# GpSimd makes every other low part at the end of each layer of a two-layer encoder

## Chip, cores and metric

The kernel runs on one core of one Trainium2 chip. The metric is the device time of one execution in microseconds (us). Three runs of the kernel before gave 1799.69, 1801.23 and 1801.38 us: the median is 1801.23 us. The trace is of one further execution, which took 1798.99 us.

## What is computed

Two encoder layers act on x, 256 tokens of 1024 channels. In each, a token mixer (two attention branches, gates, an output projection) is added to x, and then a product-key expert layer (PEER) is added to x. The PEER layer is what matters here:

```
u = expert_down[eidx]; vv = expert_up[eidx]          # 128 experts of 16384 for each token
act = gelu(einsum('td,thkd->thk', xc, u))
out = einsum('thk,thkd->td', g * act, vv)             # g: softmax over the chosen scores
x = x + out
```

The second layer starts with `rms_norm(x, norm_mix[1])` and the projection `h @ w_in[1]`, so it needs x complete.

## The kernel before

**Units.** All weights go through one stream (class `Stream`, line 156) of 602 units of 128 x 1024 float32, 301 for each layer: 66 of projections, 128 of expert_down, and 107 blocks of expert_up. I number the blocks of a layer by k, from 0 to 106; block k is unit up0 + k. A block is 128 rows of expert_up, ordered by need, and `blocks_of` (line 332) lists which of the two halves of the tokens (chunks 0 and 1) use it: blocks 90 to 98 serve both, blocks 99 to 106 serve chunk 1 alone.

**Parts.** Every unit is split in two parts, because a float32 product is made of three products of reduced parts. `_prep` (line 191) is the life of a unit: wait for its data `raw`; ScalarE (ACT) copies it into the high part `wh` (line 199); then the low part `wl = raw - wh` is made (line 203), by VectorE (DVE), or by GpSimd (POOL) where the flag `gpsimd` is set, which it is during the top-k stage; then the load of a later unit is asked for. `wh` and `wl` have 4 buffers each, so the parts of block k + 4 wait until TensorE (PE) is done with block k.

```
        engine, req = ((self.nc.vector, ("v", 1.14)), (self.nc.gpsimd, ("g", 2.5)))[self.gpsimd]   # line 200
        t = yield req
        ...
        self.splits.append(engine.tensor_sub(lo, r, h.bitcast(F32)).ins.name)
        ...
        self.load(u + self.depth)
```

**Loads.** A block of expert_up is gathered by an indirect DMA that GpSimd issues (`rows`, line 1272). Four blocks of ten land in `raw` buffers, six in free stretches of the tile `act`. `depth` is 10 during the blocks and goes back to 4 (`AHEAD`) at k = 87 (line 1461), so from then on the gather of block k + 4 is the next thing in the program after the low part of block k.

**Blocks.** `block` (line 1389) does, for each chunk, six matmuls of 512 columns (line 1401): two of the activations' high part with `wh`, two of it with `wl`, two of the activations' low part with `wh`. The activations' parts come from `split_rows`: high by ScalarE (line 1288), low by VectorE (line 1290). In front of block 97 stands `make_up` (line 1411): a block under `tc.If` for the rare rows that were missed. Every engine reads a flag there (line 1416) and branches; the body isn't entered in these runs. After block 98 chunk 0 is complete, and `norm_lane` (line 379) adds it to x and normalizes it for the next layer (lines 387, 390, 393, 397, 400, 357 to 360, 406), with a transpose on TensorE (line 368) and two parts of the result (lines 372 and 374). The last three blocks, 104 to 106, run in half-blocks of three matmuls: first all three for columns 0 to 511, then all three for columns 512 to 1023. Then comes `first_half` (line 462) of the next layer, or, in the last layer, `store_lane` (line 409).

**Order.** Each engine executes its instructions in program order. The program order is set while the kernel is built: the class `Lanes` (line 71) keeps one clock for each engine and lets generators ("lanes") emit their next instruction when the clock of that engine is near enough to TensorE's; each `yield ("v", 1.14)` is a cost on an engine's clock. SyncE (SP) issues the plain loads.

Of the kernel before, what the change touches and what calls it, by code (L numbers as in the profile page):

```python
# [70 lines left out]
class Lanes:  # L71
# [8 lines left out]
    def __init__(self):  # L80
        self.clk = {"p": 0.0, "v": 0.0, "s": 0.0, "g": 0.0}
        self.lanes = []
        self.stuck = 0
        self.urgent = 0
# [71 lines left out]
class Stream:  # L156


    def __init__(self, nc, pool, srcs, lanes):
        self.nc, self.pool, self.srcs, self.lanes = nc, pool, srcs, lanes  # L160
        self.raw, self.parts, self.ready = {}, {}, {}
        self.nd = self.np = self.want = 0
        self.ahead = self.depth = AHEAD
        self.gpsimd = False
        self.busy, self.pooled, self.splits = set(), [], []
        self.rows = None

# [23 lines left out]
    def _prep(self, u):  # L191
        self.load(u)
        while u not in self.raw:
            yield None
            self.load(u)
        yield ("s", 0.97)
        r = self.raw.pop(u)
        h = self.pool.tile([128, UNIT], F32R, name="wh", bufs=AHEAD)
        self.nc.scalar.activation(h, r, AF.Copy)  # L199
        engine, req = ((self.nc.vector, ("v", 1.14)), (self.nc.gpsimd, ("g", 2.5)))[self.gpsimd]  # L200
        t = yield req
        lo = self.pool.tile([128, UNIT], F32R, name="wl", bufs=AHEAD)
        self.splits.append(engine.tensor_sub(lo, r, h.bitcast(F32)).ins.name)  # L203
        self.ready[u] = t - 0.05
        self.parts[u] = (h, lo)
        self.busy.discard(u)
        self.load(u + self.depth)
# [19 lines left out]
def encoder_kernel(ctx, tc, x_in, wts, downs, ups, gains, gate_bias, qk_norm, rpb, sink, skeys, consts, sums, out,  # L227
# [91 lines left out]
    def bcast_row(src, off, n):  # L319
        return bass.AP(tensor=src.tensor, offset=src.offset + off, ap=[[0, 128], [1, n]])  # L320
# [3 lines left out]
    def preload(func):  # L324
        nc.scalar.activation(tiny[:, 1:2], tiny[:, 0:1], func)  # L325
# [6 lines left out]
    def blocks_of(l):  # L332


        seq = []
        for r, (_, _, cap, ea, sb) in enumerate(LISTS):
            both = [(l, r, b, (0, 1)) for b in range(sb, ea)]
            one = [(l, r, b, (0,)) for b in range(sb)] + [(l, r, b, (1,)) for b in range(ea, cap)]
            if r:
                seq += [(l, None, i, (0, 1)) for i in range(WHOLE[0], sum(WHOLE))]  # L340
                one, end = one[:sb], one[sb:]
            while both or one:
                for x in (both, one):
                    if x:
                        seq.append(x.pop(0))
        return seq + end
# [6 lines left out]
    st = Stream(nc, wpool, srcs, lanes)  # L353
# [25 lines left out]
    def norm_lane(ch, adds, gain, xn, key, halves=(0, 1)):  # L379

        sc = nst[:, ch]
        for k in halves:
            c = slice(k * 512, (k + 1) * 512)
            xs = x[:, ch, c]
            if adds:
                yield ("v", vcost(512))
                nc.vector.tensor_add(xs, xs, adds[k])
                give(adds[k], "a")
            yield ("s", scost(512))
            nc.scalar.activation(xn[:, c], xs, AF.Square, accum_out=sc[:, k:k + 1])  # L390
            if k == 0:
                yield ("v", 0.1)
                nc.vector.tensor_scalar(sc[:, 2:3], sc[:, 0:1], 1.0 / D, EPS, op0=OP.mult, op1=OP.add)
        if halves[-1] == 0:
            return
        yield ("v", 0.15)
        nc.vector.scalar_tensor_tensor(sc[:, 3:4], sc[:, 1:2], 1.0 / D, sc[:, 2:3], op0=OP.mult, op1=OP.add)
        lanes.urgent += 2
        yield ("s", 0.2)
        nc.scalar.activation(sc[:, 4:5], sc[:, 3:4], AF.Sqrt)  # L400
        yield ("v", 0.8)
        newton(sc[:, 3:4], sc[:, 4:5], sc[:, 5:6], sc[:, 6:7])
        for k in range(2):
            c = slice(k * 512, (k + 1) * 512)
            t = yield ("v", 0.68)
            nc.vector.scalar_tensor_tensor(xn[:, c], x[:, ch, c], sc[:, 4:5], gain[:, c], op0=OP.mult, op1=OP.mult)
            lanes.add(transposed_parts(ch, k, xn[:, c], key, t), first=True)

    def store_lane(ch, k, acc):
        c = slice(k * 512, (k + 1) * 512)  # L410
        yield ("v", vcost(512))
        nc.vector.tensor_add(x[:, ch, c], x[:, ch, c], acc)  # L412
        give(acc, "a")
        nc.sync.dma_start(out[ch * 128:(ch + 1) * 128, c], x[:, ch, c])
# [57 lines left out]
    u = 0  # L472
    acc_first = None

    for l in range(depth):
# [858 lines left out]
        up0 = u + 12 + 128  # L1334
        seq = blocks_of(l)
# [53 lines left out]
        def block(n, ch, halves=(0, 1), last=False):  # L1389
            h, lo = st.get(n)  # L1390
            main_need(("ga", n))
            v = ring[n]
            w = slice(ch * 128, (ch + 1) * 128)
            lh, ll = v[:, 0, w], v[:, 1, w]
            first = [(ch, hf) not in begun for hf in range(2)]
            begun.update((ch, hf) for hf in halves)

            def emit():
                for a, r in ((lh, h), (lh, lo), (ll, h)):
                    for hf in halves:  # L1400
                        nc.tensor.matmul(oacc[ch][hf], a, r[:, hf * 512:(hf + 1) * 512],  # L1401
                                         start=first[hf] and a is lh and r is h, stop=last and a is ll)

            main(emit, 0.705 * len(halves), n)

        def next_split(n):

            if n < up0 + len(seq):
                lanes.add(split_rows(n, halves_of(TTf, 4 + n % 4)), prio=1)
# [32 lines left out]
        for k, (_, r, b, chs) in enumerate(seq[:-TAIL]):  # L1442
            if k == last[0] - 1:
                make_up()
            for ch in chs:
                block(u, ch, last=k == last[ch])
            if k == 60 and l + 1 < depth:
                nc.sync.dma_start(afl[:, 0:D], bcast_row(gains, 2 * (l + 1) * D, D))
            if k == last[0]:
                preload(AF.Sqrt)  # L1450
                for x_ in [x_ for x_ in done if x_[0] == "T1"]:
                    del done[x_]
                if l + 1 < depth:
                    lanes.add(norm_lane(0, oacc[0], afl[:, 0:D], afl[:, D:2 * D], "T1"), first=True)
                else:
                    for hf in range(2):
                        lanes.add(store_lane(0, hf, oacc[0][hf]), first=True)
            if k == 1:
                st.ahead = AHEAD
            if k == len(seq) - 20:  # L1460
                st.depth = AHEAD
            st.finish(u)
            u += 1
            next_split(u + 2)
# [109 lines left out]
```

## Time and profile before

| what | value |
|---|---|
| median of 3 runs | 1801.23 us |
| the profiled execution | 1798.99 us |
| its span, first to last instruction | 1797.2 us |
| TensorE busy | 1771.5 us (99% of the span) |
| VectorE busy | 1438.8 us (80%) |
| ScalarE busy | 1096.4 us (61%) |
| GpSimd busy | 577.5 us (32%) |
| low parts made by VectorE / by GpSimd | 570 / 32 |

All times of the trace are microseconds from the start of the span. A row of the timeline is one instruction, or several alike (x4) that follow each other: start, duration of all, engine, line of the kernel, operation, output and inputs. In square brackets stands the idle time of the engine in front of it and what ended that. Matmuls overlap, so the duration of a row can reach into the next one. Layer 0 ends near 904 us, layer 1 near 1793 us.

### The profile page before, as it was taken

The page shows a single profiled execution, that of the slowest core. Times are in us where ns is not written, and L with a number is a line of the kernel's source. Part 1 is how long each engine was busy: PE and PEld are TensorE (multiplying, and loading weights), DVE is VectorE, ACT ScalarE, POOL GpSimd, SP SyncE. Part 2 cuts the span into 40 slices and gives each one's busy share as a digit, 9 for nine tenths or more (in the row PEclk, how much of TensorE's full clock was granted, in tenths as well). Part 3 has the DMA queues.
Part 4 walks back from the last instruction along what each step waited for, and adds up shares of the span by engine and source line. Part 5 has one row for each costly group of instructions (what it writes and reads, how often), then busy time and mean ns, then how long its engine had stood idle before and what let it go on. Part 6 is the DMA issues. An engine that isn't in the chain of part 4 may idle for free. (4 is left out here: it accounts for less than half of the span.)

```text
span 1797.2 us, 38047 instructions
## 1 busy us (share of the span) xinstructions
PE 1771.5 (99%) x14646; PEld 1634.2 (91%) x14646; DVE 1438.8 (80%) x3278; ACT 1096.4 (61%) x1788; POOL 577.5 (32%) x480
## 2 busy tenths in 40 slices
PE   8999999999999999999999999999999999999998
PEld 7889899999999998888778998999999999988886
DVE  6986799988878967776689768999888788677665
ACT  5675545666667646665646755556666676466654
POOL 0000160000037867755200003500000577677551
PEclk9999999999999999999999999999999999999999
DMA  7535556544458879998664355565444677899983
GB/s 262 162 106 170 160 155 190 174 143 153 143 179 251 237 243 353 358 337 287 200 211 145 112 167 164 155 186 176 142 147 152 192 243 237 253 358 357 322 286 133
DMA packets 130519, 377.42 MB, mean 210 GB/s; under 512 B 17552, under 2 KB 43792, under 8 KB 130320
## 3 DMA queue, kind: packets, MB, share of 16 engines
q1 hardware_dynamic: 90288, 239.28, 43.6%
q0 software_dynamic: 40032, 135.54, 20.7%
q8 instruction: 119, 1.95, 0.5%
q14 instruction: 80, 0.66, 0.1%
HBM read 342.00 MB, written 32.75 MB: 209 GB/s over the span
## 5 line engine op out<-in xcount | busy, mean ns | idle before, releaser
L203 DVE TENSOR_TENSOR wl<-raw,wh 128x1024 fp32r<-128x1024 f32 x444 | 541.7, 1223 | 141.6 <-ACT wh L199 131.6
L199 ACT ACTIVATE wh<-raw 128x1024 fp32r<-128x1024 f32 x476 | 502.6, 1057 | 217.8 <-PE bank L1401 58.5
L1367 PE MATMUL bank<-TT,wh 128*128 128x256 f32 x2048 | 592.0, 289 | 0.0
L1368 PE MATMUL bank<-TT,wh 128*128 128x256 f32 x2048 | 578.9, 283 | 0.0
L1369 PE MATMUL bank<-TT,wl 128*128 128x256 f32 x2048 | 578.4, 282 | 0.0
L1368 PEld LDWEIGHTS bank<-TT,wh 128*128 128x128 f32 x2048 | 392.1, 191 | 0.0
L1369 PEld LDWEIGHTS bank<-TT,wl 128*128 128x128 f32 x2048 | 391.9, 191 | 0.0
L1367 PEld LDWEIGHTS bank<-TT,wh 128*128 128x128 f32 x2048 | 391.5, 191 | 0.3
L1401 PE MATMUL bank<-wh,TT 128*128 128x512 f32 x1296 | 349.2, 390 | 3.4 <-DVE TT L1290 2.2
L1212 POOL DMA_INDIRECT rows<-act,rank x240 | 278.1, 1159 | 114.7 <-issue 60.3
L1401 PEld LDWEIGHTS bank<-wh,TT 128*128 128x128 f32 x1296 | 242.6, 188 | 56.6 <-DVE TT L1290 4.7
L888 POOL IOTA act<- 128x128 uint32 (+2 forms) x6 | 2.0, 332 | 890.5 <-PE bank L368 408.7
L203 DVE TENSOR_TENSOR wl<-act,wh 128x1024 fp32r<-128x1024 f32 x126 | 154.3, 1225 | 77.7 <-ACT wh L199 77.5
L1401 PE MATMUL bank<-wl,TT 128*128 128x512 f32 x648 | 200.8, 389 | 1.0 <-issue 1.0
L199 ACT ACTIVATE wh<-act 128x1024 fp32r<-128x1024 f32 x126 | 133.6, 1061 | 96.8 <-PE bank L1401 87.9
L1272 POOL DMA_INDIRECT act<-in_ups_dram,act x118 | 130.8, 1108 | 89.4 <-DVE TT L1290 36.7
L1401 PEld LDWEIGHTS bank<-wl,TT 128*128 128x128 f32 x648 | 121.6, 188 | 26.7 <-issue 1.4
L448 PE MATMUL bank<-TT,wh 128*128 128x256 f32 x448 | 130.1, 290 | 1.5 <-ACT raw_ka L577 1.0
L450 PE MATMUL bank<-TT,wh 128*128 128x256 f32 x448 | 126.6, 283 | 0.0
L451 PE MATMUL bank<-TT,wl 128*128 128x256 f32 x448 | 126.6, 283 | 0.0
L1072 ACT ACTIVATE oh<-oh 128x1024 f16<-128x1024 f16 (+2 forms) x108 | 101.4, 955 | 11.5 <-DVE oh L1069 10.4
L1109 ACT ACTIVATE act<-bank 128x288 f32<-128x288 f32 (+31 forms) x152 | 52.2, 347 | 92.0 <-PE bank L1096 87.8
(268 smaller groups left out, 2936.6 us busy)
## 6 DMA issues: line engine op xcount, KB each, us to landing
raw<-in_downs_dram SPq DMA_DIRECT2D x256, 512.0 KB, 3.8
raw<-in_wts_dram SPq DMA_DIRECT2D x132, 512.0 KB, 4.1
act<-rows SPq DMA_DIRECT2D x100, 129.0 KB, 5.2
act<-rows SPq DMA_DIRECT2D x98, 64.5 KB, 5.2
act<-in_ups_dram SPq DMA_DIRECT2D x8, 512.0 KB, 7.5
raw<-in_ups_dram SPq DMA_DIRECT2D x8, 512.0 KB, 6.2
rows<-act,rank POOLq DMA_INDIRECT x240
act<-in_ups_dram,act POOLq DMA_INDIRECT x118
```

Source lines behind the costliest of these rows:

```text
L199: self.nc.scalar.activation(h, r, AF.Copy)
L203: self.splits.append(engine.tensor_sub(lo, r, h.bitcast(F32)).ins.name)
L448: nc.tensor.matmul(o, wh, rh, start=first and i == 0 and pc == 0, stop=False, skip_group_check=True)
L450: nc.tensor.matmul(o, wh, rl, start=False, stop=False, skip_group_check=True)
L451: nc.tensor.matmul(o, wl, rh, start=False, stop=last and i == len(kcs) - 1 and pc == 1, skip_group_check=True)
L1072: nc.scalar.activation(el, ej, AF.Copy, scale=LOW)
L1212: snd = nc.gpsimd.indirect_dma_start(byrank[r], bass.IndirectOffsetOnAxis(ap=rank[:, i:i + 1], axis=0), afl[:, i * ROW:(i + 1) * ROW], None)
L1272: nc.gpsimd.indirect_dma_start(w, None, ups_rows, bass.IndirectOffsetOnAxis(ap=num, axis=0), element_offset=l * 16384 * D)
L1367: nc.tensor.matmul(o, lh, TT[:, :, 0, kc, :], start=kc == 0, stop=False)
L1368: nc.tensor.matmul(o, lh, TT[:, :, 1, kc, :], start=False, stop=False)
L1369: nc.tensor.matmul(o, ll, TT[:, :, 0, kc, :], start=False, stop=kc == 7)
L1401: nc.tensor.matmul(oacc[ch][hf], a, r[:, hf * 512:(hf + 1) * 512], start=first[hf] and a is lh and r is h, stop=last and a is ll)
```

## The change

```diff
@@ class Stream: __init__
         self.gpsimd = False
+        self.also = set()
@@ class Stream: _prep
-        engine, req = ((self.nc.vector, ("v", 1.14)), (self.nc.gpsimd, ("g", 2.5)))[self.gpsimd]
+        engine, req = ((self.nc.vector, ("v", 1.14)), (self.nc.gpsimd, ("g", 2.5)))[self.gpsimd or u in self.also]
@@ the loop over the blocks of expert_up
             if k == len(seq) - 20:
                 st.depth = AHEAD
+
+                st.also |= set(range(up0 + len(seq) - 10, up0 + len(seq) + 3, 2))
             st.finish(u)
```

`len(seq)` is 107. In layer 0 the set holds the units of blocks 97, 99, 101, 103 and 105 and the first and third unit of layer 1, which continue the numbers as 107 and 109: seven low parts go from VectorE to GpSimd. In layer 1 it holds blocks 97, 99, 101, 103 and 105; units 107 and 109 don't exist there. Nothing else is edited.

## Rows read from the trace of the kernel before

**Rows 1.** Busy time by stretch: sum of PE, PEld, DVE, ACT, POOL.

```profile
890.00:910.00 20.00, 16.65 (x72) 12.14 (x71) 17.42 (x33) 12.95 (x27) 0.00 (x0) 1.00 0.41 131
1700.00:1760.00 60.00, 60.00 (x267) 49.69 (x266) 39.65 (x53) 35.70 (x54) 33.78 (x30) 1.00 0.87 289
1760.00:1797.20 37.20, 31.62 (x136) 24.90 (x134) 21.18 (x31) 17.41 (x27) 3.10 (x3) 0.97 0.28 99
```

**Rows 2.** Timeline of TensorE where layer 0 ends: its waits.

```profile
896.70 1.32 PE L368 MATMUL bank<-cst,act 128*128 128x128 f32 x8 [0.84 <-DVE act L406]
...
899.89 0.73 PE L1401 MATMUL bank<-wh,TT 128*128 128x512 f32 x2 [1.42 <-DVE TT L1290]
901.23 0.73 PE L1401 MATMUL bank<-wh,TT 128*128 128x512 f32 x2 [0.38 <-DVE TT L1290]
...
907.05 0.50 PE L428 MATMUL bank<-wl,TT 128*128 128x512 f32 x1 [0.33 <-DVE wl L203]
```

**Rows 3.** Timeline of VectorE, same place.

```profile
897.23 1.22 DVE L203 TENSOR_TENSOR wl<-act,wh 128x1024 fp32r<-128x1024 f32 x1
898.36 1.28 DVE L374 TENSOR_TENSOR TT<-bank,TT 128x512 fp32r<-128x512 f32 x2
899.56 0.28 DVE L1290 SCALAR_TENSOR_TENSOR TT<-act,TT 128x128 fp32r<-128x128 f32 x1
```

**Rows 4.** Groups by line and shape, GpSimd: busy, mean ns of one, idle before.

```profile
L203 POOL TENSOR_TENSOR wl<-raw,wh 128x1024 fp32r<-128x1024 f32 x32 | 76.9, 2411 | 55.5 <-ACT wh L199 55.5
```

**Rows 5.** Timeline of GpSimd: gathers of blocks 101, 103 and 104 of layer 0.

```profile
862.99 0.94 POOL L1272 DMA_INDIRECT raw<-in_ups_dram,act  x1 [0.30 <-issue]
...
867.18 0.94 POOL L1272 DMA_INDIRECT raw<-in_ups_dram,act  x1 [0.30 <-issue]
874.01 0.94 POOL L1272 DMA_INDIRECT act<-in_ups_dram,act  x1 [5.89 <-DMA raw<-in_ups_dram,act]
```

**Rows 6.** Timeline of ScalarE: wh of blocks 97, 99, 105, then the norm's root.

```profile
874.52 1.06 ACT L199 ACTIVATE wh<-act 128x1024 fp32r<-128x1024 f32 x1 [1.35 <-PE bank L1401]
...
879.96 1.06 ACT L199 ACTIVATE wh<-act 128x1024 fp32r<-128x1024 f32 x1 [1.35 <-PE bank L1401]
...
893.75 1.05 ACT L199 ACTIVATE wh<-act 128x1024 fp32r<-128x1024 f32 x1
...
894.89 0.19 ACT L400 ACTIVATE nst<-nst 128x1 f32<-128x1 f32 x1
```

**Rows 7.** GpSimd's queue at the branch, 866 to 874 us: count, ns, start.

```profile
L1416 POOLq COMPARE_BRANCH  x1: 45/45/45, 866.9 to 866.9; - x1
L1416 POOLq INC_SWDGE_SEM  x1: 311/311/311, 872.8 to 872.8; - x1
```

**Rows 8.** DMA, 872.5 to 882 us, 40 slices of 0.24 us: GB/s.

```profile
GB/s 0 69 0 0 0 0 0 0 0 0 0 0 0 190 103 121 121 293 448 397 379 242 207 276 293 293 345 293 310 207 310 345 414 328 414 241 86 35 0 0
```

**Rows 9.** Timeline of TensorE: first use of wl of 101, 103; layer 1: 101, 103, 105.

```profile
892.03 0.61 PE L1401 MATMUL bank<-wl,TT 128*128 128x512 f32 x2
...
894.77 0.62 PE L1401 MATMUL bank<-wl,TT 128*128 128x512 f32 x2
...
1784.86 0.62 PE L1401 MATMUL bank<-wl,TT 128*128 128x512 f32 x2
...
1787.58 0.62 PE L1401 MATMUL bank<-wl,TT 128*128 128x512 f32 x2
...
1789.39 0.39 PE L1401 MATMUL bank<-wl,TT 128*128 128x512 f32 x1
```

**Rows 10.** Timeline in the top-k stage: VectorE and GpSimd.

```profile
239.50 0.53 DVE L968 TENSOR_TENSOR act<-act 128x32 f32<-128x32 f32 x5
...
253.91 4.77 POOL L203 TENSOR_TENSOR wl<-raw,wh 128x1024 fp32r<-128x1024 f32 x2 [2.00 <-ACT wh L199]
...
255.44 3.55 DVE L968 TENSOR_TENSOR act<-act 128x32 f32<-128x32 f32 x5
```

**Rows 11.** Timeline of ScalarE at the end of layer 1: wh of 97, 99.

```profile
1766.30 1.06 ACT L199 ACTIVATE wh<-act 128x1024 fp32r<-128x1024 f32 x1 [1.35 <-PE bank L1401]
...
1771.73 1.06 ACT L199 ACTIVATE wh<-act 128x1024 fp32r<-128x1024 f32 x1 [1.35 <-PE bank L1401]
```

## The prediction

> **What bounds the kernel now.** I read the busy time by stretch first. TensorE sets the time: from 1700 to 1760 us it is busy for all 60 us, and in the 20 us where layer 0 ends it is idle for 20 - 16.65 = 3.35 us while VectorE works for 17.42 [rows 1]. So a change pays only where TensorE waits. The timeline of TensorE names these waits: 0.84 us in front of the transposes of the norm (for VectorE's line 406), 1.42, 0.38 and, in a third row that repeats the pattern, 0.37 us for the low parts of the activations (line 1290), 0.33 us for a low part of weights: 3.34 us together, all for VectorE [rows 2]. The timeline of VectorE shows why: low parts of weights (1.14 us each, from 897.23 to the next start at 898.36) stand in one queue with the norm's work [rows 3]. After 1760 us TensorE is busy for 31.62 of 37.20 us [rows 1]; the last 4 us of that are the last add and store, which the change doesn't touch.
>
> **Part 1: what is removed.** VectorE loses 7 x 1.14 = 8.0 us near 900 us and 5 x 1.14 = 5.7 us near 1790. What that can give back is no more than the 3.34 us of waits; where no wait is for VectorE it gives nothing.
>
> **Part 2: what is added.** Twelve subtractions on GpSimd, 2.41 us each by the 32 it makes already [rows 4]. GpSimd has time for them: no instruction from 890 to 910 us [rows 1]. Its time is not the price; its order is.
>
> **Part 3: what is queued behind them.** GpSimd also issues the gathers. In the program the gather of block k + 4 follows the low part of block k. So long as VectorE makes that part, GpSimd's queue holds nothing but gathers and runs ahead: the gather of 101 starts at 862.99, that of 103 at 867.18 [rows 5], though wh of 97 and 99 are ready only at 874.52 + 1.06 = 875.58 and 879.96 + 1.06 = 881.02 [rows 6]. With the low parts of 97, 99, 101, 103 in the queue, each blocks GpSimd until its wh is there, and the gathers behind it wait. Layer 0, with 0.3 us between instructions of GpSimd and 0.94 for issuing a gather [rows 5]:
> - part 97 from 875.6 to 878.0; gather 101 at 878.3 (15.3 us later than now), gather 102 at 879.6;
> - part 99 from 881.0 to 883.4; gather 103 at 883.7 (16.5 us later);
> - then the branch. GpSimd passes it only when its gathers have landed (the row that corrects the semaphores starts at 872.8, 5.6 us after gather 103 [rows 5, 7]), and gather 104 starts 874.01 - 867.18 = 6.83 us after gather 103 [rows 5]. So gather 104 is at 890.5 instead of 874.01;
> - part 101 behind it, 891.5 to 893.9. TensorE uses it at 892.03 [rows 9]: 1.9 us late;
> - gathers 105 at 894.2 and 106 at 895.4; part 103 from 896.4 to 898.8, wanted at 894.77 [rows 9] + 1.9: 4.0 us late in all.
>
> The norm is hit by another way. wh of 105 now starts at 893.75, and the root of the norm's variance stands behind it on ScalarE, 1.14 us later, at 894.89 [rows 6]. That wh must now wait for gather 105 to land. How long a gather takes alone no row shows. Bounds: three start one after another from 874.01 on [rows 5], and their traffic lies in slices 14 to 37, 875.6 to 881.2 [rows 8]: a third of that is 1.9 us, so 1.6 + 1.9 = 3.5 us at least; at most the 5.6 us of gather 103, which had others in front. The root is then at 894.2 + 3.5 + 1.1 = 898.8 or 894.2 + 5.6 + 1.1 = 900.9: 3.9 to 6.0 us late, and with it the transposes, which TensorE has in its order ahead of blocks 104 to 106. This includes the 4.0 us of the parts; it isn't added to them. I take the middle, 5.0 us.
>
> **Part 4: two engines that stop each other.** In the top-k stage five small additions of VectorE take 0.53 us, but 3.55 us while two subtractions run on GpSimd, from 255.44 until just after the second ends at 253.91 + 4.77 = 258.68 [rows 10]. So VectorE stands still for what is left of a subtraction when its own work has the same kind of operands. Here part 105 starts when wh of 105 ends, 0.1 us ahead of the root; VectorE's chain behind the root (four tiny instructions, about 1 us, then line 406) would run into its 2.41 us: 2.4 - 1.1 = 1.3 us more. The bounds are 0 (only additions were seen to stall) and a whole 2.4.
>
> [...]
>
> **Part 5: what is given back.** Behind the transposes VectorE has two parts fewer (105 and 107), 2.3 us, but the two results of line 374 still stand ahead of the first line 1290 [rows 3]. Of the 1.42 + 0.38 + 0.37 us I take 1.0 back; bounds 0 and 2.2. Part 109 and unit 107 I cost at nothing, since TensorE then has six us of the first half to do; without that cover a part blocks chunk 1's norm for up to 2.4 us. Layer 0: 5.0 + 1.3 - 1.0 = 5.3 us.
>
> **Part 6: the end of layer 1.** The same queue: wh of 97 ready at 1767.36, of 99 at 1772.79 [rows 11], so part 97 until 1769.8, part 99 until 1775.2, gather 103 at 1775.5, gather 104 at 1782.3 (the same 6.83), part 101 from 1783.2 to 1785.6 against 1784.86 [rows 9], gathers 105 and 106 at 1785.9 and 1787.1, part 103 from 1788.1 to 1790.5 against 1787.58: 2.9 us late. wh of 105 ends at 1785.9 + 3.5 + 1.1 = 1790.5 or, with 5.6, at 1792.6; its part takes 2.4 more, to 1792.9 or 1795.0. TensorE wants it at 1789.39 [rows 9]: 3.5 to 5.6 us late, middle 4.5. Nothing follows that could take it up. No norm of a next layer is here, so there is nothing to give back.
>
> **Sum.** 5.3 + 4.5 = 9.8 us on the profiled 1798.99: 1808.8. The median lies 1801.23 - 1798.99 = 2.24 us above that execution, so I predict 1811.0 us. With every bound low (gathers land in 3.5 us, and the branch with them, gather 104 then 4.7 us after 103) part 103 is 2.3 us late in layer 0 and all of that is given back, and part 105 2.2 us late in layer 1: +2.2, 1803.4. With every bound high: 6.0 + 2.4 + 2.4 and 5.6 + 2.4, together +18.8, 1820.0.
>
> **Rivals.**
> - *The relief counts and the gathers aren't late*: VectorE's waits of 3.34 us go, 1801.23 - 3.3 = 1797.9. For it: TensorE's waits there are all for VectorE. Against it: it needs gathers 101 to 106 ahead of part 97 in GpSimd's queue, and line 207 stands behind line 203. It decides with the start of gather 105: by about 886 us nothing of ScalarE is late. Chance 0.12; two fifths of that past the bound below. That the set is filled too late to act is excluded: at k = 87 parts are asked for up to block 91, and the first in the set is 97.
> - *Late, but mostly hidden*: the low bounds, 1803.4. For it: gathers alone may land fast. Chance 0.14.
> - *VectorE stands still*: GpSimd's parts stop VectorE not once but at each place where its work is on the path: lines 406 and 1290 in layer 0, the norm of chunk 1 behind part 109, line 1290 at the end of layer 1; about two more subtractions' length, 2 x 2.4 = 4.8 us on the forecast, 1815.8. For it: the 3.55 us. Against it: VectorE is idle between blocks, and TensorE has blocks in hand. Chance 0.20.
>
> **How the numbers follow.** The forecast has 0.54. A measurement of this kernel tells 0.2% (3.6 us) from no change. Below 1797.6 lies 0.05 (part of the first rival); between 1797.6 and 1804.8 the rest of it, 0.07, and 0.10 of the second: 0.17; above, 0.78. The range goes from 1802.0, past the low bounds, to 1819.0, near the sum of all high ones; the first rival and the far ends of the others are the 2 in 10 outside.
>
> **What would show it.** In the timeline of GpSimd: gather 101 behind a subtraction near 878 us, gather 104 near 890, wh of 105 on ScalarE waiting for a gather near 898; the transposes of line 368 near 903 instead of 896.70; TensorE waiting for GpSimd's line 203 at blocks 101 and 103 in both layers. The forecast is wrong if gather 105 still starts before about 886 us, if TensorE's waits near 900 us sum to less than 3.34, or if VectorE's subtractions lengthen beyond 1.23 us beside GpSimd's at many places (the third rival).

## The result, and the profile after

The changed kernel takes 1822.09 us (median of 6 runs, 1817.35 to 1824.27) against 1800.51 us of the kernel before, run beside it: ratio 1.0104, 95% interval 1.0077 to 1.0131, which is 14 to 24 us slower. The direction was forecast; 1811.0 us and the range up to 1819.0 were too low. Of the runs below, two of the ten of e3, at 6079 us, and one of the 25 of the kernel before beside it, at 3249 us, were far slower than the rest, and the ratios leave such runs out.

The profiled execution took 1821.63 us, with a span of 1819.8 us against 1797.2. Lines of the changed kernel stand one higher than before (203 is 204, 1290 is 1291, 1416 is 1417). Of the 22.6 us between the spans, 3.26 lie ahead of the change: wh of block 97, which nothing of the change touches, starts at 877.78 instead of 874.52 [rows 6]. (In the traces of e1, e2, e3, e5, e11, e12 and e13 it starts between 873.64 and 875.88, so this differs from execution to execution.) So I measure from that row on.

The busy time by stretch, in the columns of [rows 1]:

```profile
890.00:910.00 20.00, 11.29 (x43) 7.74 (x41) 14.66 (x16) 11.40 (x22) 12.79 (x7) 0.81 0.59 196
910.00:930.00 20.00, 15.42 (x61) 11.47 (x61) 12.87 (x23) 6.67 (x12) 3.27 (x2) 0.85 0.34 106
```

From 890 to 910 us TensorE was idle for 3.35 us before; now it is for 20 - 11.29 = 8.7 us. The granted clock of the stretch, 1.00 before, is 0.81. VectorE works less, 14.66 us instead of 17.42, as the change says; it isn't what TensorE gets.

The timeline of TensorE where layer 0 ends, the rows that answer to [rows 2]:

```profile
896.61 0.73 PE L1402 MATMUL bank<-wl,TT 128*128 128x512 f32 x2 [0.63 <-POOL wl L204]
...
902.39 1.15 PE L1402 MATMUL bank<-wl,TT 128*128 128x512 f32 x2 [1.92 <-POOL wl L204]
...
911.42 1.97 PE L369 MATMUL bank<-cst,act 128*128 128x128 f32 x8 [7.02 <-DVE act L407]
...
923.00 0.50 PE L429 MATMUL bank<-wl,TT 128*128 128x512 f32 x1 [0.56 <-POOL wl L204]
...
926.62 0.51 PE L429 MATMUL bank<-wl,TT 128*128 128x512 f32 x1 [1.95 <-DVE wl L204]
```

The reader is to see that the waits for VectorE at line 1290 (1.42, 0.38, 0.37) behind the transposes are gone, and that larger ones stand in other places: TensorE waits for GpSimd at blocks 101 and 103, 7.02 us in front of the transposes, and in chunk 1's half for low parts that were not late before.

The timeline of GpSimd shows the queue of Part 3 (before, the gathers of [rows 5] ran ahead):

```profile
881.47 0.96 POOL L1273 DMA_INDIRECT raw<-in_ups_dram,act  x1 [0.16 <-issue]
...
886.88 0.96 POOL L1273 DMA_INDIRECT raw<-in_ups_dram,act  x1
893.19 0.94 POOL L1273 DMA_INDIRECT act<-in_ups_dram,act  x1 [5.34 <-DMA raw<-in_ups_dram,act]
894.15 2.40 POOL L204 TENSOR_TENSOR wl<-raw,wh 128x1024 fp32r<-128x1024 f32 x1
896.71 1.76 POOL L1273 DMA_INDIRECT act<-in_ups_dram,act  x1 [0.16 <-issue]
...
905.79 2.35 POOL L204 TENSOR_TENSOR wl<-act,wh 128x1024 fp32r<-128x1024 f32 x1 [3.45 <-ACT wh L200]
908.21 2.36 POOL L204 TENSOR_TENSOR wl<-raw,wh 128x1024 fp32r<-128x1024 f32 x1
920.25 2.70 POOL L204 TENSOR_TENSOR wl<-raw,wh 128x1024 fp32r<-128x1024 f32 x1 [9.68 <-ACT wh L200]
```

In square brackets "issue" means that the engine waited for nothing that the profile shows. With the 3.26 us taken off, gather 101 starts at 878.2 (forecast 878.3), 103 at 883.6 (883.7), 104 at 889.9 (890.5) and 105 at 893.4 (894.2). The queue was read rightly to the microsecond. What came behind it was not. The timeline of ScalarE (wh of 105 and the norm's root, [rows 6] before) and of VectorE (a subtraction beside part 101, the norm's tiny instructions of chunk 0, then one of chunk 1):

```profile
904.66 1.06 ACT L200 ACTIVATE wh<-act 128x1024 fp32r<-128x1024 f32 x1 [4.97 <-DMA act<-in_ups_dram,act]
905.62 0.19 ACT L401 ACTIVATE nst<-nst 128x1 f32<-128x1 f32 x1
```

```profile
894.06 3.58 DVE L204 TENSOR_TENSOR wl<-raw,wh 128x1024 fp32r<-128x1024 f32 x1 [1.57 <-ACT wh L200]
...
906.04 2.13 DVE L359 SCALAR_TENSOR_TENSOR nst<-nst 128x1 f32<-128x1 f32 x1
908.20 0.16 DVE L360 TENSOR_TENSOR nst<-nst 128x1 f32<-128x1 f32 x1
908.39 2.19 DVE L361 SCALAR_TENSOR_TENSOR nst<-nst 128x1 f32<-128x1 f32 x1
...
921.76 1.20 DVE L398 SCALAR_TENSOR_TENSOR nst<-nst 128x1 f32<-128x1 f32 x1 [1.05 <-ACT act L391]
```

Two things stand in them. Gather 105, issued at 896.71, lets its wh start only at 904.66: 7.95 us, where the forecast's upper bound was 5.6. And instructions on 128 single elements take 2.13 and 2.19 us, each until a GpSimd part ends (905.79 + 2.35 = 908.14 and 908.21 + 2.36 = 910.57), while line 360, which starts at 908.20, between the two parts, takes 0.16.

The end of layer 1: the timeline of TensorE (before: [rows 9]), one row of VectorE, and the granted clock in the last stretches, in the columns of [rows 1]:

```profile
1806.21 0.73 PE L1402 MATMUL bank<-wl,TT 128*128 128x512 f32 x2 [1.60 <-POOL wl L204]
...
1809.93 1.22 PE L1402 MATMUL bank<-wh,TT 128*128 128x512 f32 x2 [0.35 <-DVE TT L1291]
1810.95 0.63 PE L1402 MATMUL bank<-wl,TT 128*128 128x512 f32 x1
...
1815.32 0.39 PE L1402 MATMUL bank<-wh,TT 128*128 128x512 f32 x1
```

```profile
1807.17 2.70 DVE L1291 SCALAR_TENSOR_TENSOR TT<-act,TT 128x128 fp32r<-128x128 f32 x2
```

```profile
1800.00:1805.00 5.00, 4.62 (x20) 3.10 (x18) 3.45 (x4) 2.41 (x4) 4.51 (x4) 1.00 0.81 275
1805.00:1810.00 5.00, 2.88 (x7) 1.53 (x7) 4.94 (x4) 2.72 (x5) 3.52 (x2) 0.70 0.35 118
1810.00:1815.00 5.00, 5.00 (x14) 3.80 (x15) 2.11 (x4) 0.00 (x0) 0.00 (x0) 0.61 0.01 4
```

### The profile page after: what moved, and what is told of

Its sections match the earlier page's. It is cut to its first block, busy times and chain, and to the rows that moved or that the text cites. A ratio compares the mean times of both kernels' runs of the same rounds, so it can differ in the third digit from the quotient of the medians.

```text
span 1819.8 us, 38048 instructions
## 1 busy us (share of the span) xinstructions
PE 1779.4 (98%) x14646; PEld 1639.2 (90%) x14646; DVE 1448.4 (80%) x3266; ACT 1096.8 (60%) x1788; POOL 605.5 (33%) x492
## 3 DMA queue, kind: packets, MB, share of 16 engines
q8 instruction: 119, 1.95, 0.5%
## 4 chain that ended last, share of the span: by engine, by line
PE 82%; DMA 5%; issue 5%; POOL 3%; DVE 2%; ACT 2%; SPq 0%; POOLq 0%; ACTq 0%; DVEq 0%
PE bank L1368 14%; PE bank L1369 13%; PE bank L1370 13%; PE bank L1402 13%; PE bank L449 4%; PE bank L451 4%; PE bank L452 4%; DMA act<-in_ups_dram,act 3%; PE bank L428 3%; PE bank L430 3%; PE bank L429 3%; PE bank L1091 2%; PE bank L1094 2%; PE bank L1097 2%; POOL act L1273 1%
## 5 line engine op out<-in xcount | busy, mean ns | idle before, releaser
L1402 PE MATMUL bank<-wh,TT 128*128 128x512 f32 x1296 | 353.4, 394 | 5.9 <-PEq L1417 1.8
L204 DVE TENSOR_TENSOR wl<-act,wh 128x1024 fp32r<-128x1024 f32 x120 | 149.4, 1245 | 73.4 <-ACT wh L200 73.1
L204 POOL TENSOR_TENSOR wl<-raw,wh 128x1024 fp32r<-128x1024 f32 x38 | 91.6, 2416 | 65.5 <-ACT wh L200 65.3
```

## Experiments

Three theories stood after the traces were compared. **Order**: the gathers lose their lead because parts that must wait stand ahead of them in GpSimd's queue. **Stops**: a part on GpSimd and an instruction of VectorE stop each other. **Landing**: a late gather shares the DMA engines with the next layer's weights, which are loaded from about 891 us on (in the trace of SyncE the first such load stands at 891.39; before, at 886.28, when the gathers had landed by 881.2 [rows 8]).

The table gives for every kernel the time from the start of wh of block 97 to the norm's root on ScalarE, from there to the transposes of chunk 0 on TensorE, and from there to TensorE's first product behind the transposes of chunk 1; then, in layer 1, from wh of block 97 to the start of the last product. The column "excess" is the sum of the four less that of the kernel before; "by the ratio" is the measured ratio less 1, times the time of the kernel before in the same batch. All of it is from timelines of single executions. How far two of them can differ is seen from the two kernels that ran twice (e1 and e12, e7 and e13): by up to 0.3 us in the first, second and fourth column, by 0.9 and 1.6 us in the third.

| kernel | to the root | to the transposes | to chunk 1's product | layer 1, to the last product | excess, us | by the ratio, us |
|---|---|---|---|---|---|---|
| before | 20.37 | 1.81 | 15.96 | 26.47 | 0 | 0 |
| after | 27.84 | 5.80 | 17.82 | 32.89 | 19.7 | 18.7 |
| e1_ahead_only | 20.17 | 1.81 | 16.89 | 25.94 | 0.2 | -2.5 |
| e2_parts_ahead | 24.14 | 1.83 | 18.04 | 29.62 | 9.0 | 12.2 |
| e3_queue_only | 23.50 | 1.81 | 16.81 | 30.64 | 8.2 | 10.6 |
| e5_clock_kept | 27.25 | 5.82 | 17.71 | 33.36 | 19.5 | 18.0 |
| e4_four_only | 26.95 | 3.06 | 16.61 | 31.07 | 13.1 | 14.5 |
| e6_loads_held | 24.65 | 3.77 | 18.61 | 34.47 | 16.9 | 16.5 |
| e7_four_ahead | 22.20 | 2.80 | 14.62 | 28.89 | 3.9 | -4.5 |
| e9_pin_no_wait | 20.80 | 1.81 | 15.96 | 26.83 | 0.8 | 1.4 |
| e11_held_and_four | 24.66 | 3.47 | 15.98 | 31.01 | 10.5 | 13.0 |
| e12_ahead_again | 20.30 | 1.81 | 15.95 | 25.74 | -0.8 | -1.3 |
| e13_four_ahead_again | 22.06 | 2.79 | 16.17 | 29.20 | 5.6 | 4.1 |

e4, e6, e7 and e9 ran on a chip on which the kernel before takes 1935.68 us; the time it adds lies outside these stretches, as e9's row shows, so the stretches can be compared and the totals only by the ratio.

**The control: earlier gathers alone.** The kernel before, with the depth of the gathers kept at ten for seven blocks longer, so that the gathers up to block 106 stand ahead of part 97.

```diff
-            if k == len(seq) - 20:
+            if k == len(seq) - 13:
                 st.depth = AHEAD
```

> The kernel before with the gathers asked for ten blocks ahead until block 94 instead of 87, so that those of blocks 101 to 106 stand ahead of the low part of block 97 in the program. All low parts stay with VectorE. Both theories: GpSimd's queue ran ahead anyway, so the time is that of the kernel before within 2 us; this is the control for the next run.

1799.58 us against 1800.13, ratio 0.9986, interval 0.9969 to 1.0004: no difference that can be told. Earlier gathers bring the kernel before nothing, so they can be used to take the queue out of the change.

**Stops without the queue.** The changed kernel with the same earlier gathers; all twelve parts stay on GpSimd.

```diff
-            if k == len(seq) - 20:
+            if k == len(seq) - 13:
                 st.depth = AHEAD
-
+            if k == len(seq) - 20:
                 st.also |= set(range(up0 + len(seq) - 10, up0 + len(seq) + 3, 2))
```

> The changed kernel with the same earlier gathers: the twelve low parts are on GpSimd, but no gather stands behind one. If the order in GpSimd's queue is the whole loss (queue theory), the time falls back to that of the kernel before or 3 us under it (1797 to 1801). If GpSimd's subtractions also stop VectorE's instructions with two inputs in SBUF (stop theory), the norm between the layers still loses about 4 us at its tiny instructions and chunk 1 about 3, less some 1 to 3 given back, and the end of layer 1 about 1: 1803 to 1809, with VectorE's line 359 or 361 near 2 us in the trace.

1812.66 us, ratio 1.0068 (1.0045 to 1.0090): half of the loss or more is left (9.0 of 19.7 us by the stretches, 12.2 of 18.7 by the ratio) although no gather is late. It is also more than the 1803 to 1809 us that I gave the stops, and they fell elsewhere: lines 359 and 361 took 0.16 us each here, and line 1291, ahead of the norm's root, was stopped instead. (The profiled execution is one of the longer ones, 1819.68 us; beside the trace of the kernel before, it falls back by some 8 us between 1600 and 1750 us, with 627 matmuls there against 666, where the change does nothing.) The timeline of VectorE, GpSimd and TensorE:

```profile
888.76 2.39 POOL L204 TENSOR_TENSOR wl<-raw,wh 128x1024 fp32r<-128x1024 f32 x1 [3.92 <-ACT wh L200]
888.91 2.39 DVE L1291 SCALAR_TENSOR_TENSOR TT<-act,TT 128x128 fp32r<-128x128 f32 x1 [0.86 <-ACT TT L1289]
...
896.79 2.98 POOL L204 TENSOR_TENSOR wl<-act,wh 128x1024 fp32r<-128x1024 f32 x1 [0.52 <-ACT wh L200]
897.48 2.44 DVE L1291 SCALAR_TENSOR_TENSOR TT<-act,TT 128x128 fp32r<-128x128 f32 x1
...
899.97 0.73 PE L1402 MATMUL bank<-wh,TT 128*128 128x512 f32 x2 [1.84 <-DVE TT L1291]
900.02 0.20 ACT L401 ACTIVATE nst<-nst 128x1 f32<-128x1 f32 x1 [3.31 <-DVE nst L398]
```

Line 1291 takes 0.28 us alone [rows 3] and 2.4 us beside a part; the instruction behind it in VectorE's order, line 398, is what the root waits 3.31 us for. Part 105 itself, at 896.79, took 2.98 us instead of 2.4: each engine stops the other.

**The queue without the parts.** VectorE makes all parts; in the places of the change GpSimd subtracts one column of wh from one of raw, so that it waits for the same things, and is then free.

```diff
-        engine, req = (...)[self.gpsimd or u in self.also]
+        engine, req = (...)[self.gpsimd]
...
+        if u in self.also:
+            pin = self.pool.tile([128, 1], F32, name="pin", bufs=1)
+            self.nc.gpsimd.tensor_sub(pin, r[:, 0:1], h[:, 0:1].bitcast(F32))
```

> VectorE makes all low parts, as before; for the twelve units of the change GpSimd executes a subtraction of one column of wh and raw in the place where the change has the whole part. So the gathers stand behind a wait for wh, as in the changed kernel, but nothing takes 2.4 us and nothing stops VectorE for long. Queue theory: the gathers are late all the same, the one of 105 by 12 us or more, and its block lands at 895 to 897 us instead of in good time: 1 to 4 us slower than before. If the waits for wh alone made the loss, it would be 10 us or more; if only the subtractions' own length and stops count, 0 to 1 us.

1809.99 us (median of eight runs), ratio 1.0059 (1.0036 to 1.0082): 6.5 to 15 us, more than I gave it. The timeline of GpSimd, VectorE and ScalarE:

```profile
876.36 1.23 DVE L204 TENSOR_TENSOR wl<-act,wh 128x1024 fp32r<-128x1024 f32 x1 [1.16 <-ACT wh L200]
876.41 1.22 POOL L207 TENSOR_TENSOR pin<-act,wh 128x1 f32<-128x1 f32 x1 [12.97 <-ACT wh L200]
...
888.84 0.94 POOL L1276 DMA_INDIRECT act<-in_ups_dram,act  x1 [4.65 <-DMA raw<-in_ups_dram,act]
...
891.05 0.95 POOL L1276 DMA_INDIRECT act<-in_ups_dram,act  x1
...
897.61 1.06 ACT L200 ACTIVATE wh<-act 128x1024 fp32r<-128x1024 f32 x1 [1.57 <-DMA act<-in_ups_dram,act]
...
898.79 0.19 POOL L207 TENSOR_TENSOR pin<-act,wh 128x1 f32<-128x1 f32 x1 [4.44 <-ACT wh L200]
```

One column takes 0.19 us at 898.79, where VectorE is idle (from 897.17 to 898.99), and 1.22 us where VectorE's own subtraction has begun 0.05 us earlier: here GpSimd is the one that is stopped. Gather 105 stands at 891.05, and its wh starts 6.56 us later. So the order, with the landing that comes with it, costs about 8 us without any part on GpSimd: 4 at the boundary, 4 at the end of layer 1.

**The clock.** In the changed kernel TensorE's granted clock is 0.50 from about 902.5 to 916 us. It fell already behind the wait of 1.92 us at block 103 (1.00 from 900 to 902 us, 0.50 from 903 to 904), and it stays there through the idle 7.02 us. To see what that costs, 56 matmuls on the table `iota2`, whose result the transposes overwrite, stand ahead of the transposes. (The table holds index numbers by then, not zeros, since line 510 has filled it.)

```diff
+        if key == "T1" and ch == 0 and k == 0 and u:
+            z2 = iota2.rearrange("p a b -> p (a b)")
+            for _ in range(56):
+                nc.tensor.matmul(b[:, 0:256], z2[:, 0:128], z2, start=True, stop=True)
```

> The changed kernel with 56 matmuls of 256 columns on zeros (6.3 us at 0.11 us each) on TensorE in front of the transposes between the layers, where it was idle for 7.0 us; their result is overwritten. If the lower clock after the idle time (granted clock 0.50 from 905 to 915 us in the changed kernel) costs time on the path, the eight transposes and the nine matmuls behind them run at full speed again and the time falls by 1.5 to 2.5 us. If the wait for VectorE behind the transposes hides it, the time stays within 1 us of the changed kernel.

1820.06 us, ratio 1.0100 (1.0063 to 1.0137): no difference to the changed kernel that the runs can tell. The interval is 13 us wide, so the 1.5 to 2.5 us that were asked about are decided by the stretches and not by the total. The busy time by stretch of the changed kernel, then of this one, in the columns of [rows 1]:

```profile
905.00:910.00 5.00, 0.00 (x0) 0.00 (x0) 4.06 (x4) 3.33 (x7) 4.14 (x2) 0.50 0.18 71
910.00:915.00 5.00, 3.58 (x13) 3.10 (x14) 4.88 (x9) 1.19 (x2) 0.56 (x1) 0.50 0.35 108
```

```profile
900.00:905.00 5.00, 5.00 (x45) 4.25 (x45) 3.79 (x4) 3.59 (x7) 3.89 (x2) 1.00 0.36 136
905.00:910.00 5.00, 4.05 (x28) 2.85 (x25) 4.96 (x9) 1.20 (x2) 0.85 (x1) 1.00 0.34 105
```

The clock was kept at 1.00, and from the transposes to the first product of the next layer it took 6.48 us (906.71 to 913.19) instead of 7.27 (911.42 to 918.69). The 0.8 us are a consequence of the waits, not their cause, and most of them are waited away again in chunk 1 (17.71 us in all against 17.82).

**Four parts only.** Parts 105, 107 and 109 go back to VectorE; the queue is the changed kernel's.

```diff
-                st.also |= set(range(up0 + len(seq) - 10, up0 + len(seq) + 3, 2))
+                st.also |= set(range(up0 + len(seq) - 10, up0 + len(seq) - 3, 2))
```

> The changed kernel, with GpSimd making only the parts 97, 99, 101 and 103 of each layer's end (105, 107 and 109 go back to VectorE). In the changed kernel's trace the parts 103 to 109 run beside the two tiny instructions of the norm that took 2.13 and 2.19 us in place of 0.16 (4.0 us at the norm) and beside chunk 1's work (2.9 us). If those are stops of VectorE by a GpSimd part: part 103 still lies at the first of them and 105 no longer at the second, so one of the two stops goes (some 2 us) and chunk 1's 2.9 us go too: ratio to the kernel before 1.0075 to 1.009, some 1815 us. If VectorE was late there for another reason (the late root alone): ratio as with the change, 1.010.

Ratio 1.0075 (1.0050 to 1.0101), the lower end of what the stops were to leave. In its trace the tiny instructions of both norms take 0.15 and 0.16 us each. Both stops of chunk 0's norm went, not one: the parts beside it in the changed kernel were 105 and 107, not 103 and 105 as I had written. From the root to the transposes it takes 3.06 us instead of 5.80. Chunk 1 takes 1.2 us less, which is no more than two executions of one kernel differ by there. What remains over the kernel before from root to transposes, 1.25 us, is an order of VectorE: with four parts fewer on VectorE's clock the planner puts part 105 ahead of the norm's tiny instructions (964.92 before 966.27), where it stood behind line 406 (897.23 [rows 3]).

**The landing.** The four loads of the next layer's weights wait until wh of 105 is made; all parts as in the change.

```diff
             else:
+                if self.nd >= self.hold and self.gate is None:
+                    return
...
-                self.nc.sync.dma_start(r, src)
+                d = self.nc.sync.dma_start(r, src)
+                if self.hold <= self.nd < self.hold + 4:
+                    self.tc.add_manual_dep(d.ins, self.gate, ...)
...
-        self.nc.scalar.activation(h, r, AF.Copy)
+        a = self.nc.scalar.activation(h, r, AF.Copy)
+        if u == self.hold - 2:
+            self.gate = a.ins.name
```

Here `hold` is the first unit of layer 1.

> The changed kernel, with the four loads of the next layer's weights that ran beside the last gathers of the first boundary held until the first part of unit 105 is made. If gather 105 took 7.84 us to land because it shared the DMA engines with those loads: it lands in 5.0 to 6.0 us, the norm's root comes 2 to 3 us earlier, and the time falls by some 2 us, to about 1820. If the time is that of issuing (VectorE's subtraction beside the gather's descriptors) or of the gathers sharing with one another: it lands in 7 to 8 us as before and the time is the changed kernel's, 1822.

The timelines of GpSimd (gather 105) and ScalarE (wh of 105), first of e4, whose loads are not held, then of this kernel, on the same chip:

```profile
956.14 1.76 POOL L1273 DMA_INDIRECT act<-in_ups_dram,act  x1 [0.16 <-issue]
...
963.83 1.06 ACT L200 ACTIVATE wh<-act 128x1024 fp32r<-128x1024 f32 x1 [4.77 <-DMA act<-in_ups_dram,act]
```

```profile
956.15 0.95 POOL L1281 DMA_INDIRECT act<-in_ups_dram,act  x1
...
960.55 1.06 ACT L206 ACTIVATE wh<-act 128x1024 fp32r<-128x1024 f32 x1 [2.14 <-DMA act<-in_ups_dram,act]
```

7.69 us became 4.40 us (7.95 in the changed kernel, not 7.84 as I had written), and the root comes 3.19 us earlier than in the changed kernel. Not all of the 3.3 us are the loads. Issuing this gather took 1.76 us in e4, where a subtraction of VectorE was under way when it began (953.77 + 3.30 = 957.07), and 0.95 us here. The next run has the long issue and the held loads; there it is 5.18 us. So 0.8 us are the issue and 2.5 us the loads, which the profile counts on the same 16 DMA engines (in the changed kernel, from 890 to 912 us, 2.16 MB of loads in 30.3% of these engines' time and 1.80 MB of gathers in 25.1%). The end of layer 1, where no further weights are loaded, agrees: with the long issue the gather takes 5.07 us there in e4 (1933.75 to 1938.82) and at most 5.45 us in the changed kernel (1800.77 to 1806.22).

The boundary gained 4.4 us in the trace, more than the expected 2, because the norm met one part of GpSimd and not two (3.77 instead of 5.80 us from the root to the transposes). That is an effect of the edit itself: unit 107 is one of the four whose loads are held, its wh waits 1.18 us for its data, and its part starts only when the tiny instructions are done (964.44):

```profile
966.32 3.15 POOL L212 TENSOR_TENSOR wl<-raw,wh 128x1024 fp32r<-128x1024 f32 x1 [2.28 <-ACT wh L206]
```

The ratio, 1.0085 (1.0044 to 1.0126), is too wide to show it: the end of layer 1, which this edit leaves alone, was 1.6 us longer in this execution.

**Both.** Loads held and four parts only.

> The changed kernel with both edits that were tried alone: the four loads of the next layer's weights held until the first part of unit 105, and only the parts 97, 99, 101 and 103 on GpSimd. From the wait at the branch to the transposes the changed kernel took 25.52 us and the kernel before 14.06. If the excess of 11.46 us is the gathers' place in the queue (4.0 us), the shared landing of gather 105 (some 3.4 us) and the stops at the norm (4.0 us), and these add: the first alone is left, transposes some 17.5 to 18.5 us after the wait, nothing lost in chunk 1, ratio 1.003 to 1.005. If holding the loads only moves the transfer into something else: 20 us or more, ratio 1.007 or more.

1811.18 us, ratio 1.0072 (1.0047 to 1.0097). From the wait at the branch (883.35) to the transposes it took 20.0 us, not 17.5 to 18.5; chunk 1 lost nothing (15.98 us). The timelines of GpSimd and ScalarE show gather 105 and its wh:

```profile
893.74 1.76 POOL L1281 DMA_INDIRECT act<-in_ups_dram,act  x1 [0.16 <-issue]
...
898.92 1.06 ACT L206 ACTIVATE wh<-act 128x1024 fp32r<-128x1024 f32 x1 [2.38 <-DMA act<-in_ups_dram,act]
```

The root stands at 24.66 us, as in e6: 4.3 us are left to the order, as expected. That the two agree so closely is chance: the gather starts 18.51 us after wh of 97 here and 19.28 in e6, and lands in 5.18 and 4.40 us. The missing 1.7 us lie between root and transposes (3.47 against 1.81): as in e4, VectorE makes part 105 there, at 900.01, ahead of the norm's tiny instructions from 901.40 on. So order and landing add about as expected, and in place of the stops there is a smaller delay, which comes from the planner and not from GpSimd. The end of layer 1, 4.5 us longer than before, which I had left out of the sum, makes the ratio higher than expected.

**No wait in the queue.** As e3, but the one-column subtraction reads a constant tile, so that GpSimd waits for nothing.

```diff
-            self.nc.gpsimd.tensor_sub(pin, r[:, 0:1], h[:, 0:1].bitcast(F32))
+            self.nc.gpsimd.tensor_sub(pin, self.still, self.still)
```

> VectorE makes all second parts, as before; GpSimd does in the places of the change a one-column subtraction of a constant tile that has long been there, so that it waits for nothing. If the cost of the order is the wait for the first part that stands ahead of the later gathers: no difference to the kernel before, ratio 0.998 to 1.001. If it is the instructions themselves between the gathers (their issue, or GpSimd being stopped by VectorE): as with the one-column subtraction that waited, ratio 1.005.

Ratio 1.0007 (0.9974 to 1.0041), and all four stretches within 0.5 us of the kernel before. The instructions between the gathers cost nothing; their wait for wh does.

**Four parts behind the gathers.** First on the slower chip, then again beside the control, with more runs.

```diff
-            if k == len(seq) - 20:
+            if k == len(seq) - 13:
                 st.depth = AHEAD
-
-                st.also |= set(range(up0 + len(seq) - 10, up0 + len(seq) + 3, 2))
+            if k == len(seq) - 20:
+                st.also |= set(range(up0 + len(seq) - 10, up0 + len(seq) - 3, 2))
```

> The changed kernel with the gathers ahead of the parts (as in the earlier run with all parts) and only the parts 97, 99, 101 and 103 on GpSimd. Neither a queue of gathers nor a part beside the norm or chunk 1 is left; what remains are the stops of VectorE's subtraction of the next block's rows beside the parts (0.28 to 2.4 us each, three or four times a layer end). If those alone reach the path: 3 to 5 us over the kernel before, ratio 1.0015 to 1.003. If all of the earlier run's excess came from the parts at the norm and in chunk 1: no difference, ratio 0.999 to 1.001. If stops anywhere in these stretches count: 1.005 or more.

> The kernel before with the earlier gathers alone (VectorE makes all parts), beside the next kernel. The first look gave 0.9986, its interval just over 1. If the gathers that wait behind the branch cost the kernel before anything: ratio 0.997 to 0.999. If what they bring is hidden by VectorE's and ScalarE's own work: 0.9995 to 1.0005.

> The gathers ahead of the parts, and GpSimd making the parts 97, 99, 101 and 103 alone. The first look gave 0.9977 with an interval on both sides of 1; its profiled execution lost 2.16 us before the last chunk behind one stopped subtraction and nothing at the boundary. If that is all there is: 1 to 2 us over the earlier gathers alone, ratio 1.000 to 1.001. If relieving VectorE of four parts brings what the change was to bring: below the earlier gathers alone, ratio 0.997 or less.

The first measurement gave 0.9977 (0.9941 to 1.0014), which couldn't tell. Beside the control (e12: 1798.11 us, 0.9993, 0.9977 to 1.0008, which can't tell its two cases apart) the same kernel takes 1804.89 us, ratio 1.0023 (1.0009 to 1.0036), more than the 1 to 2 us expected. So four parts on GpSimd, with no queue behind them, cost 2 to 6 us; about 1 us of it is part 105 ahead of the norm, as in e4 (2.79 against 1.81). The timeline of VectorE and TensorE shows two of the places:

```profile
893.50 2.39 DVE L1291 SCALAR_TENSOR_TENSOR TT<-act,TT 128x128 fp32r<-128x128 f32 x1
...
895.95 1.19 PE L1402 MATMUL bank<-wh,TT 128*128 128x512 f32 x4 [0.99 <-DVE TT L1291]
...
1788.99 2.63 DVE L1291 SCALAR_TENSOR_TENSOR TT<-act,TT 128x128 fp32r<-128x128 f32 x2
1791.47 1.20 PE L1402 MATMUL bank<-wh,TT 128*128 128x512 f32 x4 [2.16 <-DVE TT L1291]
```

A VectorE that is relieved of a 1.14 us part and stopped for 2.1 us beside it has less time, not more. No version here beats the kernel before by more than the runs can tell.

## Why the prediction was right and wrong

The loss of 13.3 us at the boundary (51.46 - 38.14, the sums of the first three columns) comes apart as follows: 4.28 us from the order, with the loads held (the root in e6 and e11); 3.19 more with the loads beside the gather (27.84 - 24.65); 3.99 from the stops at the norm (5.80 - 1.81); 1.86 in the stretch behind the transposes, the one that varies most between executions. The end of layer 1 lost 6.42. The forecast had 5.3 and 4.5.

- **Parts 1 and 2** held. The waits for line 1290 went, and a part takes 2.4 us on GpSimd. Its time was not the price.
- **Part 3, the queue**, held in every start time of layer 0, and in the size of what the queue itself costs: the root 4.28 us late, in the bounds of 3.9 to 6.0. **The step that failed is the bound on the landing of gather 105**, "at most the 5.6 us of gather 103, which had others in front". It took 7.95 us. I had read how long gathers land among gathers, and not asked what else runs some 18 us later than now: the loads of the next layer's weights, and VectorE's subtraction, beside which the issue took 1.76 us instead of 0.94. With the loads held it is 4.40 us (e6) and 5.18 (e11, with the long issue), inside the bounds. The branch behaved as read (5.34 us of waiting).
- **Part 4, the stop**, was the right mechanism and the wrong count: 1.3 us with an upper bound of one subtraction, 2.4. There were two, one behind the other, 3.99 us. I had counted part 105 and costed part 107, which follows it at once, at nothing. The copies of 105, 106 and 107 follow each other on ScalarE (904.66, 905.93, 907.09), so part 107 starts 0.07 us after part 105 ends, and the tiny instructions met both; where wh of 107 was late (e6), they met one. The stop reached the smallest instructions: 0.16 us became 2.13 and 2.19 us on 128 single elements, and 0.28 became 2.4 in e2. All of these have two tensors as inputs; line 358, a reciprocal with one, took 0.16 us at 905.84, beside the part from 905.79 to 908.14. Which of the two waits is not told by their start times alone: line 204 at 894.06 took 3.58 us beside part 101, which starts at 894.15, and in e5 one at 895.72 took 3.75 beside a part that starts at 896.00.
- **Part 5** gave back what was said: from the transposes to the first product of the next layer 7.27 us instead of 8.27, 1.0 us. That it is just the 1.0 is luck: at a granted clock of 1.00 (e5) it was 6.48, so 1.8 us were given back and 0.8 lost again where 0.67 was granted on average. Nor did the results of line 374 (now 375) stay ahead of the first line 1290 (now 1291), as the prediction had it: with fewer parts on VectorE the planner put line 1291 first (911.95 before 913.28). And "part 109 and unit 107 I cost at nothing" failed: from there to chunk 1's product it took 10.55 us instead of 7.69, 2.9 us more, by the waits of 0.56 and 1.95 us for low parts and one stop of 1.20 us. Without these parts the stretch from the transposes to chunk 1's product is 16.61 us (e4) and 15.98 (e11), against 15.96 before. The cover was shorter than the six us: the wait of 1.95 us is for a part of VectorE that stands behind chunk 1's norm, and that norm was itself stopped.
- **Part 6** was sized rightly, in part by luck, and not complete. The low part of 105 was used 28.52 us after wh of 97 (1810.95 - 1782.43) instead of 23.09 (1789.39 - 1766.30): 5.4 us late, inside 3.5 to 5.6. But gather 105 started 18.34 us after that wh and not 19.6, because gather 104 came 5.60 us after 103 and not 6.83; and the low part, made by 1809.72, was not what TensorE waited for last. That was line 1291 (0.35 us at 1809.93), two of which took 2.70 us beside that part. The other 1.0 us is the clock: after the waits from 1804.6 us on TensorE was granted 0.70 and then 0.61 on average (1.00 before the waits, and 1.00 in the kernel before), and from that use to the last product it took 4.37 us, before 3.38.
- **The rivals.** That the relief counts fell: gather 105 starts at 893.4, not by 886. That it is late but mostly hidden fell too: the root comes 7.47 us late (27.84 - 20.37). That VectorE stands still at several places (chance 0.20, 1815.8 us) came true, at three of the places that it named: line 1291 in layer 0 (2.43 us at 900.06, while the norm still waited for gather 105), the norm of chunk 1, and line 1291 at the end of layer 1. The fourth, line 406 (now 407), took its 1.41 us for two as before. The sign set for this rival came too: line 204 took 3.58 us on VectorE at 894.06, 2.13 at 1799.58 and 3.59 at 1803.66, beside parts of GpSimd. The rival too was priced on top of a landing of at most 5.6 us. Had I added the 3.2 us of the landing to it, the sum would have been 1819. The error behind it is that the stops beyond the first were a rival and not a term of the sum. e2, e3 and the change show that they belong into it: 9.0 + 8.2 us against 19.7 by the stretches. By the ratios it is 12.2 + 10.6 against 18.7, so whether something comes only where both are there is not settled.

Not settled either is how e3's 4.2 us at the end of layer 1 come apart, and why the end of e6 was 1.6 us longer; neither was tried alone.

## What to carry to other kernels

Before work is moved to an engine that also issues DMAs, write down its queue: here an instruction that waited for its input took away the lead of every transfer behind it (ratio 1.0059 in e3, 1.0007 without the wait in e9), and a late transfer has to be priced among what runs on the DMA engines at its new time, not at its old one (gather 105 took 7.95 us beside the next layer's loads, 5.18 with them held). GpSimd's subtractions were not free time beside VectorE here: count each two-input instruction of VectorE that falls into their span, the tiny ones on the critical chain first (0.16 us became 2.13 and 2.19), and let the costs of queue and stops add. Here the wait was behind a chain of tiny instructions, and the engine that looked idle was the wrong place for a long subtraction.

## What was not expected of the hardware

- The stop works in both directions and for tiny instructions: GpSimd's subtraction of one column takes 0.19 us alone and 1.22 beside VectorE's subtraction (e3); VectorE's instruction on 128 elements takes 0.16 alone and 2.19 beside GpSimd's.
- Issuing a gather lengthens too, where a subtraction of VectorE is already under way when it starts; it then ends some 0.8 us after the subtraction. Gather 105 of e4 took 1.76 us in place of 0.95 (956.14 to 957.90, the subtraction until 957.07). The kernel before has it as well: 1.67 us from 861.02 to 862.69, the subtraction until 861.88. A subtraction that begins after the gather leaves it at 0.94 us (898.77 and 898.91 in the changed kernel). Why is not shown.
- A gather of 512 KB lets its reader start 4.4 us after the start of its issue when the next layer's loads are held (5.2 with the long issue), and 7.7 to 8.0 us when they run beside it, with the long issue.
